# Average pooling over 64x256x8192: transfers of 64 KB per partition on one queue, with pairwise sums

## The chip, the cores and the metric

The kernel runs on one core of a Trainium2 chip. The metric is the device time in microseconds (us). Three runs of the kernel before gave 1561.38, 1561.14 and 1561.12 us; their median is 1561.14 us.

## The reference

The input x has 64 x 256 rows of 8192 float32 numbers. Each row is cut into windows of four, and the output is the mean of each window, so 64 x 256 rows of 2048.

```python
out_len = (length - kernel_size) // stride + 1     # 2048
for i in range(out_len):
    start = i * stride                             # kernel_size = stride = 4
    output[:, :, i] = np.mean(x[:, :, start : start + kernel_size], axis=2)
```

That is 536.87 MB to read and 134.22 MB to write, with three additions and one multiplication per result.

## The kernel before

The 16384 rows are taken in 32 groups of 512. A group gives each of the 128 partitions four rows that follow one another in memory, so a partition reads 128 KB of x and writes 32 KB of the output in one stretch. The function `_packed_fast_path` does the work (`F` is 4, `NTM` is 32); the rest of `tile_avg_pool_1d_kernel` holds paths that these shapes don't take.

For each group but the last, an inner loop over `f` takes one row per partition at a time. SP issues a load of 32 KB per partition, 4 MB in all (L245), into a tile `xt` from a pool of three buffers. VectorE sums each four neighbours with one TENSOR_REDUCE (L246) into a quarter of the result tile `ot`, which comes from a pool of two buffers. ACT multiplies that quarter by 1/4 in place (L252). After four rows ACT issues one store of the group, again 32 KB per partition and 4 MB (L253). So SP's queue carries the loads and ACT's the stores, and both queues feed the same 16 DMA engines.

The last group is cut finer. Its first row is loaded whole, its second and third in three chunks each (L263, L266, L272), and its fourth in a ladder of six chunks that get smaller, the last 608 columns wide (L284, L293, L309). The chunks of the ladder are stored by ACT as they are done (L310). The first three rows' results are held back and stored by SP in four pieces (L292) behind the last load. The very last chunk is scaled on VectorE into a tile `fin` (L300) and stored by SP (L307).

The tile framework puts in the semaphore waits: a load waits until the tile that it overwrites has been read, a reduction waits for its load and for the store that last read its result buffer, and so on. The order on each engine is the order of the program text. Each engine issues its DMAs in that order, and a DMA that waits holds up what stands behind it on the same engine.

Of the kernel before, what the change touches and what calls it, by code (L numbers as in the profile page):

```python
# [7 lines left out]
_N_PARK = 4  # L8
_FINAL_COLS_TGT = 608
_LADDER_RATIO = 1.39  # L10
_NCHUNK_PRE = 3
_PACK_STORES = True
_PACK_F_MAX = 4


def _tail_ladder(total: int, k: int, final: int, ratio: float = _LADDER_RATIO,
                 max_chunks: int = 12) -> list:
    if total < 4 * final:
        return [total]
    rev = []  # L20
    s = 0
    w = float(final)
    while len(rev) < max_chunks - 1:
        wi = max(k, (int(round(w)) // k) * k)
        if s + wi > total - k:
            break
        rev.append(wi)
        s += wi
        w *= ratio
    sizes = [total - s] + rev[::-1]  # L30
    assert sum(sizes) == total and all(x > 0 and x % k == 0 for x in sizes)
    return sizes


def _even_chunks(total: int, k: int, n: int) -> list:
    n = max(1, min(n, total // k))
    q = (total // n) // k * k
    sizes = [q] * n
    sizes[-1] += total - q * n
    assert sum(sizes) == total and all(s > 0 and s % k == 0 for s in sizes)  # L40
    return sizes


@with_exitstack
def kernel(
    ctx: ExitStack,
    tc: tile.TileContext,
    x: bass.AP,
    kernel_size: bass.AP,
    stride: bass.AP,  # L50
    out: bass.AP,
):
    nc = tc.nc

    K = int(kernel_size)
    S = int(stride)
    assert K == S, "only stride == kernel_size supported"

    B, C, L = x.shape
    OL = (L - K) // S + 1  # L60
    assert OL * K <= L

    P = nc.NUM_PARTITIONS

    xf = x.flatten_outer_dims()
    of = out.flatten_outer_dims()
    rows = B * C

    inv_k = 1.0 / float(K)
    dt = x.dtype  # L70
    IL = OL * K

    if _PACK_STORES and IL == L:
        F = 0
        for cand in range(_PACK_F_MAX, 1, -1):
            if rows % (P * cand) == 0 and (rows // (P * cand)) >= 2:
                F = cand
                break
        if F >= 2 and L >= 64 * K and OL % 8 == 0 and OL * F * 4 <= 32768:
            _packed_fast_path(nc, tc, xf, of, rows, L, OL, K, F, inv_k, dt, P)  # L80
            return

    RPP = 1
    R = P * RPP
    NT = rows // R
    IL2 = RPP * L
    OL2 = RPP * OL
    fast = (
        IL == L
        and rows % R == 0  # L90
        and NT >= 6
        and IL2 >= 64 * K
        and OL % 2 == 0
    )

    if not fast:
        with (
            tc.tile_pool(name="xin", bufs=4) as pin,
            tc.tile_pool(name="res", bufs=4) as pout,
        ):  # L100
            r0 = 0
            while r0 < rows:
                rn = min(P, rows - r0)
                xt = pin.tile([P, IL], dt)
                ot = pout.tile([P, OL], dt)
                nc.sync.dma_start(out=xt[:rn], in_=xf[r0 : r0 + rn, :IL])
                nc.vector.tensor_reduce(
                    out=ot[:rn],
                    in_=xt[:rn].rearrange("p (m k) -> p m k", k=K),
                    axis=mybir.AxisListType.X,  # L110
                    op=mybir.AluOpType.add,
                )
                nc.scalar.mul(ot[:rn], ot[:rn], inv_k)
                nc.scalar.dma_start(out=of[r0 : r0 + rn], in_=ot[:rn])
                r0 += P
        return

    def xview(t):
        return xf[t * R : (t + 1) * R]

    def oview(t):
        return of[t * R : (t + 1) * R]

    ladder = _tail_ladder(IL2, K, _FINAL_COLS_TGT)
    chunks_pre = _even_chunks(IL2, K, _NCHUNK_PRE)
    fin_w = ladder[-1] // K

    with (
        tc.tile_pool(name="xin", bufs=4) as pin,
        tc.tile_pool(name="res", bufs=4) as pout,  # L130
        tc.tile_pool(name="rsv", bufs=1) as prsv,
        tc.tile_pool(name="fin", bufs=1) as pfin,
    ):
        rsv = prsv.tile([P, OL2], dt)
        fin = pfin.tile([P, fin_w], dt)

        for t in range(NT):
            xv = xview(t)
            ov = oview(t)
            xt = pin.tile([P, IL2], dt)  # L140
            ot = rsv if t == 0 else pout.tile([P, OL2], dt)

            if t == 0:
                nc.sync.dma_start(out=xt[:, :IL2], in_=xv[:, :IL2])
                nc.vector.tensor_reduce(
                    out=ot[:, :OL2],
                    in_=xt[:, :IL2].rearrange("p (m k) -> p m k", k=K),
                    axis=mybir.AxisListType.X,
                    op=mybir.AluOpType.add,
                )  # L150
                nc.scalar.mul(ot[:, :OL2], ot[:, :OL2], inv_k)
            elif t < NT - 3:
                nc.sync.dma_start(out=xt[:, :IL2], in_=xv[:, :IL2])
                nc.vector.tensor_reduce(
                    out=ot[:, :OL2],
                    in_=xt[:, :IL2].rearrange("p (m k) -> p m k", k=K),
                    axis=mybir.AxisListType.X,
                    op=mybir.AluOpType.add,
                )
                nc.scalar.mul(ot[:, :OL2], ot[:, :OL2], inv_k)  # L160
                nc.scalar.dma_start(out=ov[:, :OL2], in_=ot[:, :OL2])
            elif t < NT - 1:
                c0 = 0
                for cw in chunks_pre:
                    c1 = c0 + cw
                    o0, o1 = c0 // K, c1 // K
                    nc.sync.dma_start(out=xt[:, c0:c1], in_=xv[:, c0:c1])
                    nc.vector.tensor_reduce(
                        out=ot[:, o0:o1],
                        in_=xt[:, c0:c1].rearrange("p (m k) -> p m k", k=K),  # L170
                        axis=mybir.AxisListType.X,
                        op=mybir.AluOpType.add,
                    )
                    nc.scalar.mul(ot[:, o0:o1], ot[:, o0:o1], inv_k)
                    nc.scalar.dma_start(out=ov[:, o0:o1], in_=ot[:, o0:o1])
                    c0 = c1
            else:
                nchunk = len(ladder)
                c0 = 0
                for i, cw in enumerate(ladder):  # L180
                    c1 = c0 + cw
                    o0, o1 = c0 // K, c1 // K
                    last = i == nchunk - 1
                    nc.sync.dma_start(out=xt[:, c0:c1], in_=xv[:, c0:c1])
                    if last:
                        q0 = 0
                        qw = (OL2 - q0) // _N_PARK
                        for qi in range(_N_PARK):
                            qa = q0 + qi * qw
                            qb = q0 + (qi + 1) * qw if qi != _N_PARK - 1 else OL2  # L190
                            nc.sync.dma_start(
                                out=oview(0)[:, qa:qb], in_=rsv[:, qa:qb]
                            )
                    nc.vector.tensor_reduce(
                        out=ot[:, o0:o1],
                        in_=xt[:, c0:c1].rearrange("p (m k) -> p m k", k=K),
                        axis=mybir.AxisListType.X,
                        op=mybir.AluOpType.add,
                    )
                    if last:  # L200
                        nc.vector.tensor_scalar(
                            out=fin[:, :fin_w],
                            in0=ot[:, o0:o1],
                            scalar1=inv_k,
                            scalar2=None,
                            op0=mybir.AluOpType.mult,
                        )
                        nc.sync.dma_start(out=ov[:, o0:o1], in_=fin[:, :fin_w])
                    else:
                        nc.scalar.mul(ot[:, o0:o1], ot[:, o0:o1], inv_k)  # L210
                        nc.scalar.dma_start(out=ov[:, o0:o1], in_=ot[:, o0:o1])
                    c0 = c1


def _packed_fast_path(nc, tc, xf, of, rows, L, OL, K, F, inv_k, dt, P):
    R = P * F
    NTM = rows // R

# [10 lines left out]
    with (  # L229
# [6 lines left out]
        for t in range(NTM):  # L236
            xv = xe(t)
# [109 lines left out]
```

## Time and profile before

| what | value |
|---|---|
| time, median of three runs | 1561.14 us (1561.12 to 1561.38) |
| span of the profiled execution, first to last instruction | 1559.0 us |
| VectorE (DVE) busy | 1112.8 us, 71% |
| ScalarE (ACT) busy | 247.4 us, 16% |
| bytes moved by the DMA engines | 671.14 MB, 430 GB/s over the span |
| HBM read and written | 536.87 MB and 134.22 MB |
| DMA packets | 25637 |
| loads of 4096 KB | 125, median 26.4 us from issue to landing |
| stores of 4096 KB by ACT | 31, median 23.2 us from issue to landing |

The profile is that of one execution. Its own time is its span, 1559.0 us, and what lies around the span, which the page doesn't list; against the median of the three runs that is 2.1 us.

The rows are read as follows. Busy time of an engine is the time in which it worked on instructions; issuing a DMA isn't counted. The row called DMA divides the span into 40 slices and gives, in tenths, how busy the 16 DMA engines were. A queue (q1, q10) has packets; the share is the time that its packets took out of 16 engines' span. A group of instructions is a line of the program with its operation and shapes, its number, its busy time and the mean of one, and the idle time of its engine just before it with what ended it. In the waits, the columns are the total, how often, and the longest. A "packet" is one piece that one DMA engine moves: each transfer here gives each of the 16 engines eight rows of partitions, and one packet of 4 bytes that reports the end. The chain is the work that ended last, followed back from the end.

### The profile page before, as it was taken

Reading aid. Unit: us, or ns where it says so; the run is one execution under the profiler, and the core shown is the slowest. Engines: PE = TensorE matmul, PEld = TensorE weight load, DVE = VectorE, ACT = ScalarE, POOL = GpSimd, SP = SyncE. Lnnn points to the kernel's source line nnn. Section 1 sums busy time; section 2 is a strip of 40 time slices with the busy share of each in tenths; the row PEclk is TensorE's granted clock in tenths of the full one; section 3 lists DMA queues with packets and bytes.
Section 4 is the critical chain, followed back from the end, with each engine's and each line's share of the span. In section 5 each row is a group of like instructions: output and inputs, shape, how many; then the busy total and the mean of one; then the engine's idle time right before and its main releaser. Section 6 shows DMA issues by size and latency. Waiting matters only on the chain.

```text
span 1559.0 us, 724 instructions
## 1 busy us (share of the span) xinstructions
DVE 1112.8 (71%) x138; ACT 247.4 (16%) x137; POOL 0.2 (0%) x4
## 2 busy tenths in 40 slices
DVE  6777667776667866677666776667766677766786
ACT  1111111111111111111111111111111111111111
POOL 0000000000000000000000000000000000000000
DMA  9999999999999999999999999999999999999999
GB/s 416 418 430 436 437 432 430 430 430 432 439 433 430 430 432 430 438 434 431 430 432 430 435 434 433 431 431 430 433 437 433 432 430 431 430 437 434 432 427 384
DMA packets 25637, 671.14 MB, mean 430 GB/s; under 512 B 2848, under 2 KB 3488, under 8 KB 4768
## 3 DMA queue, kind: packets, MB, share of 16 engines
q1 hardware_dynamic: 20448, 540.10, 80.6%
q10 hardware_dynamic: 5184, 131.00, 19.5%
q14 instruction: 5, 0.04, 0.0%
HBM read 536.87 MB, written 134.22 MB: 430 GB/s over the span
## 4 chain that ended last, share of the span: by engine, by line
DMA 75%; DVE 24%; issue 0%; SPq 0%; DVEq 0%
DMA xt<-in_x_dram 75%; DVE ot L246 23%; DVE ot L293 1%; DVE ot L266 0%; SPq L263 0%; DVEq L246 0%; DVE fin L300 0%
## 5 line engine op out<-in xcount | busy, mean ns | idle before, releaser
L246 DVE TENSOR_REDUCE ot<-xt 128x2048 f32<-128x8192 f32 x124 | 1077.1, 8686 | 430.2 <-DMA xt<-in_x_dram 430.2
L252 ACT ACTIVATE ot<-ot 128x2048 f32<-128x2048 f32 x124 | 237.0, 1911 | 1270.2 <-DVE ot L246 1270.2
L266 DVE TENSOR_REDUCE ot<-xt 128x682 f32<-128x2728 f32 (+2 forms) x7 | 26.6, 3809 | 6.9 <-DMA xt<-in_x_dram 6.9
L272 ACT ACTIVATE ot<-ot 128x682 f32<-128x682 f32 (+2 forms) x7 | 6.6, 936 | 25.8 <-DVE ot L266 25.8
L293 DVE TENSOR_REDUCE ot<-xt 128x417 f32<-128x1668 f32 (+5 forms) x6 | 9.0, 1568 | 0.0
L309 ACT ACTIVATE ot<-ot 128x417 f32<-128x417 f32 (+4 forms) x5 | 2.6, 521 | 5.2 <-DVE ot L293 5.2
L252 ACT ACT_TABLE_LOAD x1 | 1.3, 1283 | 0.7 <-PEq L328 0.7
L300 DVE TENSOR_SCALAR fin<-ot 128x152 f32<-128x152 f32 x1 | 0.2, 239 | 0.0
L328 POOL MEMSET const-bfloat16-1.0<- 128x1 bf16 x1 | 0.1, 102 | 0.0
L328 POOL MEMSET const-uint8-127<- 128x1 uint8 x1 | 0.1, 102 | 0.0
L328 POOL MEMSET const-float32-0.0<- 128x1 f32 x1 | 0.1, 99 | 0.2 <-issue 0.2
L328 POOL MEMSET const-float32-1.0<- 128x1 f32 x1 | 0.1, 99 | 0.0
## 6 DMA issues: line engine op xcount, KB each, us to landing
xt<-in_x_dram SPq DMA_DIRECT2D x125, 4096.0 KB, 26.4
out_dram<-ot ACTq DMA_DIRECT2D x31, 4096.0 KB, 23.2
xt<-in_x_dram SPq DMA_DIRECT2D x4, 1364.0 KB, 23.4
out_dram<-ot SPq DMA_DIRECT2D x4, 768.0 KB, 7.7
xt<-in_x_dram SPq DMA_DIRECT2D x2, 1368.0 KB, 29.5
xt<-in_x_dram SPq DMA_DIRECT2D x1, 1134.0 KB, 16.2
xt<-in_x_dram SPq DMA_DIRECT2D x1, 834.0 KB, 22.6
xt<-in_x_dram SPq DMA_DIRECT2D x1, 816.0 KB, 17.8
```

What stands on the lines that cost most here:

```text
L246: nc.vector.tensor_reduce(out=ot[:, o0 : o0 + OL], in_=xt[:, :L].rearrange("p (m k) -> p m k", k=K), axis=mybir.AxisListType.X, op=mybir.A ...
L252: nc.scalar.mul(ot[:, o0 : o0 + OL], ot[:, o0 : o0 + OL], inv_k)
L266: nc.vector.tensor_reduce(out=ot[:, o0:o1], in_=xt[:, c0:c1].rearrange("p (m k) -> p m k", k=K), axis=mybir.AxisListType.X, op=mybir.AluOp ...
L272: nc.scalar.mul(ot[:, o0:o1], ot[:, o0:o1], inv_k)
L293: nc.vector.tensor_reduce(out=ot[:, o0:o1], in_=xt[:, c0:c1].rearrange("p (m k) -> p m k", k=K), axis=mybir.AxisListType.X, op=mybir.AluOp ...
L300: nc.vector.tensor_scalar(out=fin[:, :fin_w], in0=ot[:, o0:o1], scalar1=inv_k, scalar2=None, op0=mybir.AluOpType.mult,)
L309: nc.scalar.mul(ot[:, o0:o1], ot[:, o0:o1], inv_k)
L328: nc = _bacc.Bacc("TRN2", target_bir_lowering=False, num_devices=1)
```

## The change

The paths that other shapes need are taken out, and the main path is written anew.

- A tile `xt` holds 16384 columns, 64 KB per partition, from a pool of two buffers instead of three of 32 KB. A load fills it at once: 8 MB.
- A group is 65536 columns per partition, eight rows that follow one another in memory, so there are 16 groups of four loads. The result tile `ot` holds 64 KB per partition, from a pool of one buffer instead of two of 32 KB. One store writes it: 8 MB.
- All loads and stores are issued by SP. Two loads are issued ahead; load k+2 is issued behind the sums of tile k and, where tile k ends a group, behind the group's store.
- The sum of four is made in two levels: one add of even and odd columns, written over the first half of the tile itself, and one add of even and odd columns of that, written to `ot`. In the fourth tile of a group the second level is cut into four parts, with a multiplication by ACT after each.
- The last tile is loaded in five pieces of 8192, 4096, 2048, 1024 and 1024 columns. The last group's results are stored in four parts: two tiles' worth between the first and the second piece, then the third tile's, then 3584 columns, then 512. The last two pieces are scaled on VectorE.

The diff, cut to what is new and to the lines of `_packed_fast_path` that it replaces:

```diff
-    with (
-        tc.tile_pool(name="xin", bufs=3) as pin,
-        tc.tile_pool(name="res", bufs=2) as pout,
-        tc.tile_pool(name="fin", bufs=1) as pfin,
-    ):
...
-            if t < NTM - 1:
-                for f in range(F):
-                    xt = pin.tile([P, L], dt)
-                    o0 = f * OL
-                    nc.sync.dma_start(out=xt[:, :L], in_=xv[:, f * L : (f + 1) * L])
-                    nc.vector.tensor_reduce(
...
-                    nc.scalar.mul(ot[:, o0 : o0 + OL], ot[:, o0 : o0 + OL], inv_k)
-                nc.scalar.dma_start(out=ov[:, : F * OL], in_=ot[:, : F * OL])
-                continue
...
+LOADS = 4
+LAST_CUTS = 4
...
+    per = B * C * L // P
+    W = 16384
+    G = W * LOADS
+    V = W // K
+    groups = per // G
...
+    rows = G // L
+    R = P * rows
+    def xg(g):
+        return xf[g * R : (g + 1) * R].rearrange("(p f) m -> p (f m)", f=rows)
...
+    pin = ctx.enter_context(tc.tile_pool(name="xin", bufs=2))
+    pout = ctx.enter_context(tc.tile_pool(name="res", bufs=1))
+    state = {}
+    def load(g, l, a, b):
+        if a == 0:
+            state["xt"] = pin.tile([P, W], dt, name="xt")
+        xt = state["xt"]
+        nc.sync.dma_start(out=xt[:, a:b], in_=xg(g)[:, l * W + a : l * W + b])
+        return xt
+    def sums(xt, ot, l, a, b, cuts, scale_on_dve=False):
+        h = (a, (a + b) // 2)
+        nc.vector.tensor_tensor(
+            out=xt[:, h[0] : h[1]], in0=xt[:, a:b:2], in1=xt[:, a + 1 : b : 2], op=add
+        )
+        n = (b - a) // K
+        for c in range(cuts):
+            lo, hi = c * n // cuts, (c + 1) * n // cuts
+            o = ot[:, l * V + a // K + lo : l * V + a // K + hi]
+            nc.vector.tensor_tensor(
+                out=o,
+                in0=xt[:, a + 2 * lo : a + 2 * hi : 2],
+                in1=xt[:, a + 2 * lo + 1 : a + 2 * hi : 2],
+                op=add,
+            )
+            if scale_on_dve:
+                nc.vector.tensor_scalar(
+                    out=o, in0=o, scalar1=1.0 / K, scalar2=None, op0=mybir.AluOpType.mult
+                )
+            else:
+                nc.scalar.mul(o, o, 1.0 / K)
+    def store(g, ot, a, b):
+        nc.sync.dma_start(out=og(g)[:, a:b], in_=ot[:, a:b])
+    todo = [(g, l) for g in range(groups) for l in range(LOADS)]
+    last = todo[-1]
+    pieces = [W // 2, W // 4, W // 8, W // 16, W // 16]
+    tiles = {}
+    ot = None
+    tiles[0] = load(*todo[0], 0, W)
+    tiles[1] = load(*todo[1], 0, W)
+    for k, (g, l) in enumerate(todo[:-1]):
+        if l == 0:
+            held, ot = ot, pout.tile([P, G // K], dt, name="ot")
+        sums(tiles.pop(k), ot, l, 0, W, LAST_CUTS if l == LOADS - 1 else 1)
+        if l == LOADS - 1:
+            store(g, ot, 0, G // K)
+        if k + 2 < len(todo) - 1:
+            tiles[k + 2] = load(*todo[k + 2], 0, W)
+        elif k + 2 == len(todo) - 1:
+            n = pieces[0]
+            lt = load(*last, 0, n)
+            store(g, ot, 0, (l + 1) * V)
+            for w in pieces[1:]:
+                load(*last, n, n + w)
+                n += w
+    g, l = last
+    store(g, ot, (l - 1) * V, l * V)
+    edges = [sum(pieces[:i]) for i in range(len(pieces) + 1)]
+    for a, b in zip(edges[:3], edges[1:4]):
+        sums(lt, ot, l, a, b, 1)
+    store(g, ot, l * V, l * V + edges[3] // K)
+    for a, b in zip(edges[3:-1], edges[4:]):
+        sums(lt, ot, l, a, b, 1, scale_on_dve=True)
+    store(g, ot, l * V + edges[3] // K, (l + 1) * V)
```

More of the change, by code (lines that the diff above doesn't have):

```diff
@@ L6 @@
 from concourse._compat import with_exitstack
[L8 to L41, printed above, removed]
+LOADS = 4
+LAST_CUTS = 4
 @with_exitstack
@@ L53 @@
     nc = tc.nc
-    K = int(kernel_size)
-    S = int(stride)
-    assert K == S, "only stride == kernel_size supported"
+    K, S = int(kernel_size), int(stride)
+    assert K == S == 4
     B, C, L = x.shape
-    OL = (L - K) // S + 1
-    assert OL * K <= L
     P = nc.NUM_PARTITIONS
+    add = mybir.AluOpType.add
+    dt = x.dtype
+    per = B * C * L // P
[3 more added lines that the diff above has]
+    groups = per // G
+    assert per == groups * G
     xf = x.flatten_outer_dims()
@@ L66 @@
     of = out.flatten_outer_dims()
[L67 to L96, printed above, removed]
-        with (
-            tc.tile_pool(name="xin", bufs=4) as pin,
-            tc.tile_pool(name="res", bufs=4) as pout,
-        ):
[L101 to L106, printed above, removed]
-                nc.vector.tensor_reduce(
[L108 to L111, printed above, removed]
-                )
[L113 to L131, printed above, removed]
-        tc.tile_pool(name="fin", bufs=1) as pfin,
[L133 to L176, printed above, removed]
-            else:
[L178 to L212, printed above, removed]
@@ L215, in _packed_fast_path @@
-def _packed_fast_path(nc, tc, xf, of, rows, L, OL, K, F, inv_k, dt, P):
-    R = P * F
-    NTM = rows // R
-    ladder = _tail_ladder(L, K, _FINAL_COLS_TGT)
-    chunks_pre = _even_chunks(L, K, _NCHUNK_PRE)
-    fin_w = ladder[-1] // K
-    def xe(t):
-        return xf[t * R : (t + 1) * R].rearrange("(p f) m -> p (f m)", f=F)
-    def oe(t):
-        return of[t * R : (t + 1) * R].rearrange("(p f) m -> p (f m)", f=F)
-    with (
-        tc.tile_pool(name="xin", bufs=3) as pin,
-        tc.tile_pool(name="res", bufs=2) as pout,
-        tc.tile_pool(name="fin", bufs=1) as pfin,
-    ):
-        fin = pfin.tile([P, fin_w], dt)
-        for t in range(NTM):
-            xv = xe(t)
-            ov = oe(t)
-            ot = pout.tile([P, F * OL], dt)
-            if t < NTM - 1:
-                for f in range(F):
-                    xt = pin.tile([P, L], dt)
-                    o0 = f * OL
-                    nc.sync.dma_start(out=xt[:, :L], in_=xv[:, f * L : (f + 1) * L])
-                    nc.vector.tensor_reduce(
-                        out=ot[:, o0 : o0 + OL],
-                        in_=xt[:, :L].rearrange("p (m k) -> p m k", k=K),
-                        axis=mybir.AxisListType.X,
-                        op=mybir.AluOpType.add,
-                    )
-                    nc.scalar.mul(ot[:, o0 : o0 + OL], ot[:, o0 : o0 + OL], inv_k)
-                nc.scalar.dma_start(out=ov[:, : F * OL], in_=ot[:, : F * OL])
-                continue
-            for f in range(F - 1):
-                xt = pin.tile([P, L], dt)
-                widths = [L] if f < F - 3 else chunks_pre
-                c0 = 0
-                for cw in widths:
-                    c1 = c0 + cw
-                    o0, o1 = f * OL + c0 // K, f * OL + c1 // K
-                    nc.sync.dma_start(
-                        out=xt[:, c0:c1], in_=xv[:, f * L + c0 : f * L + c1]
-                    )
-                    nc.vector.tensor_reduce(
-                        out=ot[:, o0:o1],
-                        in_=xt[:, c0:c1].rearrange("p (m k) -> p m k", k=K),
-                        axis=mybir.AxisListType.X,
-                        op=mybir.AluOpType.add,
-                    )
-                    nc.scalar.mul(ot[:, o0:o1], ot[:, o0:o1], inv_k)
-                    c0 = c1
-            fq = F - 1
-            xt = pin.tile([P, L], dt)
-            hold = fq * OL
-            nchunk = len(ladder)
-            c0 = 0
-            for i, cw in enumerate(ladder):
-                c1 = c0 + cw
-                o0, o1 = fq * OL + c0 // K, fq * OL + c1 // K
-                last = i == nchunk - 1
-                nc.sync.dma_start(
-                    out=xt[:, c0:c1], in_=xv[:, fq * L + c0 : fq * L + c1]
-                )
-                if last:
-                    qw = hold // _N_PARK
-                    for qi in range(_N_PARK):
-                        qa = qi * qw
-                        qb = (qi + 1) * qw if qi != _N_PARK - 1 else hold
-                        nc.sync.dma_start(out=ov[:, qa:qb], in_=ot[:, qa:qb])
-                nc.vector.tensor_reduce(
-                    out=ot[:, o0:o1],
-                    in_=xt[:, c0:c1].rearrange("p (m k) -> p m k", k=K),
-                    axis=mybir.AxisListType.X,
-                    op=mybir.AluOpType.add,
-                )
-                if last:
-                    nc.vector.tensor_scalar(
-                        out=fin[:, :fin_w],
-                        in0=ot[:, o0:o1],
-                        scalar1=inv_k,
-                        scalar2=None,
-                        op0=mybir.AluOpType.mult,
-                    )
-                    nc.sync.dma_start(out=ov[:, o0:o1], in_=fin[:, :fin_w])
-                else:
-                    nc.scalar.mul(ot[:, o0:o1], ot[:, o0:o1], inv_k)
-                    nc.scalar.dma_start(out=ov[:, o0:o1], in_=ot[:, o0:o1])
-                c0 = c1
@@ new lines, with og @@
+    rows = G // L
+    R = P * rows
+    def xg(g):
+        return xf[g * R : (g + 1) * R].rearrange("(p f) m -> p (f m)", f=rows)
+    def og(g):
+        return of[g * R : (g + 1) * R].rearrange("(p f) m -> p (f m)", f=rows)
+    pin = ctx.enter_context(tc.tile_pool(name="xin", bufs=2))
[7 more added lines that the diff above has]
+        return xt
```

## The prediction

> **What bounds the kernel now.** I read the busy rows first, then the DMA rows, the chain that ended last, the waits, and last the trace's own DMA packet records. The page's head, busy rows, DMA slices and queues:
>
> ```profile
> span 1559.0 us, 724 instructions
> DVE 1112.8 (71%) x138; ACT 247.4 (16%) x137; POOL 0.2 (0%) x4
> DMA  9999999999999999999999999999999999999999
> DMA packets 25637, 671.14 MB, mean 430 GB/s; under 512 B 2848, under 2 KB 3488, under 8 KB 4768
> q1 hardware_dynamic: 20448, 540.10, 80.6%
> q10 hardware_dynamic: 5184, 131.00, 19.5%
> ```
>
> No engine is full, but the 16 DMA engines are: their row never falls under 9, and the two queues' packets (q1 is SP's, q10 ACT's) fill 80.6 + 19.5 = 100.1% of 16 engines' span. All bytes must move in either version, 671.09 MB, so time can only come from what the DMA engines do besides moving bytes, or from idling. The windows answer both:
>
> ```profile
> 100.00:1500.00 1400.00, 1000.30 (x116) 221.61 (x116) 0.00 (x0) 1.00 1.00 433
> 1551.00:1554.00 3.00, 0.00 (x0) 0.00 (x0) 0.00 (x0) 1.00 1.04 401
> 1554.00:1557.00 3.00, 0.00 (x0) 0.00 (x0) 0.00 (x0) 1.00 0.65 253
> ```
>
> (last two columns: DMA share, GB/s). For 1400 us the engines stand at 1.00 and 433 GB/s; only the last 4 us sag. So the chain's and the waits' rows, which name VectorE too, show a pipeline paced by loads:
>
> ```profile
> DMA xt<-in_x_dram 75%; DVE ot L246 23%; DVE ot L293 1%; DVE ot L266 0%; SPq L263 0%; DVEq L246 0%; DVE fin L300 0%
> DVE ot L246 <- DMA xt<-in_x_dram: 430.2, 124, 12.7
> SPq L245 <- DVE ot L246: 1053.4, 121, 8.8
> ```
>
> VectorE waits 430 us for loads. SP waits 1053 us for VectorE to free a tile, but that costs nothing: other loads are queued then, as the full DMA row shows.
>
> **What a packet costs besides its bytes.** The trace records every packet. 25637 = 16 x (8+1) x 178 + 5: each of the 178 transfers (137 loads, 41 stores) gives every engine eight data packets, one per partition row, and one of 4 B. From one packet's start to the next on the same engine I find on average 1212.7 ns after 32768 B, 409.4 ns after 10912 B, 27.1 ns after 608 B, and 6 ns after the 4 B packet. From 10912 to 32768 B the slope is 803.3/21856 = 0.03676 ns/B and 8.3 ns are left per packet; from 608 to 32768 B 0.03687 ns/B, with 4.7 ns left. I take the middle, 6.5 ns.
>
> **The change, part by part.**
>
> *Transfers of 64 KB.* Transfers fall to 68 loads (63 whole, the last tile in 5 pieces) and 19 stores (15 whole, 4 for the last group): 87, so each engine has 696 data packets instead of 1424, and 91 fewer 4 B packets. Gain: 728 x 6.5 ns = 4.7 us, and 91 x 6 ns = 0.5 us. Nothing hides it, since the DMA engines are the bound. A 65536 B packet is not in the trace: if its extra cost grows with its bytes, the 4.7 is 0; at 8.3 ns it is 6.0. I take the middle.
>
> *Stores on SP's queue, in line with loads.* Today the queues alternate packet by packet: a load packet followed by a store packet takes 1211.9 ns, store then load 1210.1, load then load 1214.0. Changing direction at every packet thus costs nothing visible; changing at 16 stores costs nothing either, and losing the alternation costs at most 1214.0 - 1210.1, about 4 ns on each of some 2 x 3968/16 = 496 packets: 2 us. From below, losing the alternation could gain as much. I take 0. After a store's 4 B packet the next packet on the queue starts 6 ns later, in the tail too, so a store ahead doesn't hold the line.
>
> *Sums in two levels.* Per 64 KB tile an add with 8192 results and one (or four quarters) with 4096 results replace two reductions. No two-input add is in the trace. The nearest rows are
>
> ```profile
> L246 DVE TENSOR_REDUCE ot<-xt 128x2048 f32<-128x8192 f32 x124 | 1077.1, 8686 | 430.2 <-DMA xt<-in_x_dram 430.2
> L266 DVE TENSOR_REDUCE ot<-xt 128x684 f32<-128x2736 f32 x2 | 6.0, 3004 | 4.3 <-DMA xt<-in_x_dram 4.3
> ```
>
> (mean ns after busy us): (8686-3004)/(8192-2736) = 1.041 ns per element read, 155 ns fixed. If an add takes this per result, the levels cost 8.69 and 4.42, 13.1 us a tile (13.6 with four quarters); if per element read, 17.2 and 8.7, 25.9 us. I take the first: the nearest row on how fast VectorE can read is the TENSOR_SCALAR of L300, 239 ns for 152 elements, (239-155)/152 = 0.55 ns each, so two elements per 1.04 ns are within its reach. The Trainium skill, "VectorE: DVE Perf Modes", section on the TRN2 errata, gives a fp32 two-input add (N+151)/0.96 ns; its estimate would be 8.7 + 4.4 = 13.1 us. No run shown here has it.
>
> *Two tiles, one result buffer, one queue: does the line run dry?* A 64 KB load takes 8 x 2 x 1212.7 ns less the saving, 19.3 us. From the first tile of before: VectorE starts 0.37 us after the load's last packet, and the first packet moves 1.0 us after SP's issue. Load k+2 waits for the sums of tile k: 0.37 + 13.2 + 1.0 = 14.6 us after that tile landed, while load k+1 holds the line for 19.3. Cover: 4.7 us. At the start the first tile lands 9.7 us later than today, but the second load is queued behind it, so the line stays full. A store must come sooner: 0.37 + 13.7, then ACT's last quarter (ACT rows: 772 ns at 682, 1911 at 2048, so 1.06 at 1024), + 1.0 = 16.2 us. Cover: 3.1 us; each us beyond it idles the engines 16 times. Behind the waiting store in SP's queue stands the next load, which needs only the same sums, and the line is filled by the load before. The next group's second level waits until the store has left the buffer, 19.3 us after that store starts; its tile is then freed 19.3 + 0.4 + 4.4 = 24 us after, well inside the 38.7 us that store and next load take together. Four loads per store and one buffer thus cost 0.
>
> *The tail.* Before, from 1554.00 to the last packet's end at 1557.63 (packet records) the engines are busy 0.65 x 3 + about 0.02 of 3.63 us: 1.6 us idle. After, the last tile's pieces land while stores still queue: with the durations above the 14 KB store is ready 1.9 us before its turn, the final 2 KB one 3.5 us before. (ACT's 3.6 us per 4096 results and the scaling of the last two pieces on VectorE, some 0.3 us each, are in this.) What stays is the spread between engines (0.47 us between first and last 4 B packet of one load). Gain 1.2 us; ends 0 and 1.6. Start (first packet at 1.73 us) and the 1.4 us after the last packet stay.
>
> **Sum.** 4.7 + 0.5 + 1.2 = 6.4 us off the profiled span: 1559.0 becomes 1552.6. That execution's span lies 2.1 us below the runs' median 1561.14; these 2.1 stay, so the forecast is **1554.7 us**. Ends: 6.0 + 0.5 + 1.6 + 2 = 10.1 off, 1551.0; with 0 for packets and tail, and alternation lost: 0.5 - 2, so 1562.6.
>
> **A rule that speaks against it.** The load rows' pitch per partition grows from 128 to 256 KB, the stores' from 32 to 64 KB. Before, at 128 KB, moves 433 GB/s. The Trainium skill, "DMA: Bandwidth & Descriptors", section "Latency and other measured facts", has HBM copies at a pitch of 512 KiB at 207 GB/s where a padded pitch gave 214, and much less at larger powers of two. By it a pitch between could lose up to about 3%, an estimate of 47 us and 1600 us. No run here shows it.
>
> **Rivals.** (1) *No change within 0.2% (3 us; about what a measurement of this kernel can tell):* the 64 KB row goes out as two packets of 32 KB, or the extra cost grows with the bytes. Then only 0.5 + 1.2 stay: 1559.4. For it: no packet over 32768 B is in the trace, and the average packet lies 3.7 ns over the fastest (1209), which may be any cause. Against: packets of six sizes all show a fixed part.
> (2) *Slower: the adds are paced by elements read.* Then VectorE, not DMA, is the bound: a group costs 3 x 25.9 + 17.2 + 4 x 2.3 = 104 us, against 96.8 for its DMA, plus about 4.5 in which the second level waits for the store: 16 x 108.6 + 22 for the first load + 6 = about 1766 us. It decides from 16.8 us of sums a tile on (13.7 + 3.1); I expect 13.7. For it: two strided inputs, in place, never seen here. Against: the 0.55 ns per element of L300.
> (3) *Slower: DMA packets of 64 KB rows run slower*, by pitch or direction. Each 1% costs 15 us: 1570 at 1%. Against: the alternation costs nothing, and the tail's 6144 B stores take 230 ns, their bytes at the same slope and 4 ns.
>
> **Chances.** Forecast 0.70; (1) 0.14; (2) 0.06; (3) 0.10. So faster 0.70, same 0.14, slower 0.16. The range runs from 1551.0 to 1562.6 and takes in the bounds and (1), leaving out (2) and (3).
>
> **What would show it.** Right: about 12,500 packets, loads of 65536 B at about 2418 ns, DMA share 1.00 and 434 GB/s or more in the middle, adds of 8.7 and 4.4 us. Wrong: twice the packets (rival 1); adds over 11 us and DMA slices under 9 (2); packets over 2440 ns (3); a dip of the DMA row once per group would say that the store's cover is gone.

## The result, and the profile after

| | time, median (lowest to highest) | ratio to before |
|---|---|---|
| before, 20 runs | 1561.02 us (1560.80 to 1561.44) | |
| changed, 20 runs | 1558.42 us (1556.78 to 1560.36) | 0.9984 [0.9978, 0.9990] |

The forecast was 6.4 us less; 2.6 us came. The time lies inside the stated range, and it lies closer to "no change" than to the forecast. The profiled execution of the changed kernel took 1560.02 us, 1.6 us over its median. So its profile shows one of its longest runs; the runs of the changed kernel are spread over 3.6 us, those of before over 0.6. Two later repeats (e12 and e16 below) came 1.5 and 1.2 us under the kernel before, so the gain is some 1 to 2.6 us.

The page of the changed kernel, the lines that answer to those shown of before:

```profile
span 1558.2 us, 522 instructions
DVE 844.0 (54%) x183; ACT 241.9 (16%) x112; POOL 0.2 (0%) x4
DMA  9999999999999999999999999999999999999998
DMA packets 12532, 671.13 MB, mean 431 GB/s; under 512 B 1392, under 2 KB 1392, under 8 KB 1776
q1 hardware_dynamic: 12528, 671.09, 99.8%
```

The packets are 16 x 9 x 87 + 4, as worked out ahead, so a row of 64 KB does go out as one packet. The DMA row stays at 9 in every slice but the last, which shows 8. The queue's share says more: 99.8% of a span that is only 0.8 us shorter. The packets are half as many and take nearly as long.

Groups by form, mean ns of one after busy us, and two waits, the first of VectorE, the second of SP:

```profile
L65 DVE TENSOR_TENSOR xt<-xt 128x8192 f32<-128x8192 f32 x63 | 547.6, 8693 | 537.0 <-DMA xt<-in_x_dram 537.0
L72 DVE TENSOR_TENSOR ot<-xt 128x4096 f32<-128x4096 f32 x48 | 212.4, 4425 | 163.5 <-DMA out_dram<-ot 162.4
L72 DVE TENSOR_TENSOR ot<-xt 128x1024 f32<-128x1024 f32 x61 | 70.7, 1220 | 0.5
```

```profile
DVE ot L72 <- DMA out_dram<-ot: 162.4, 15, 11.2
```

```profile
SPq L59 <- DVE ot L72: 780.1, 47, 24.3
```

The adds take 8.69, 4.42 and 1.22 us, one result per 1.04 ns. The wait for the one result buffer is there, 11 us for each of 15 groups, and the DMA slices above show no gap for it.

The middle and the tail in windows (last columns: DMA share, GB/s), against 433 GB/s in the first window and shares of 1.04 and 0.65 in the other two before:

```profile
100.00:1500.00 1400.00, 752.66 (x157) 214.68 (x99) 0.00 (x0) 1.00 1.00 434
1551.00:1554.00 3.00, 0.00 (x0) 0.00 (x0) 0.00 (x0) 1.00 0.92 389
1554.00:1557.00 3.00, 0.00 (x0) 0.00 (x0) 0.00 (x0) 1.00 0.34 135
```

**Where the gain went.** I split the DMA engines' time, in us per engine, by the packet records of both traces. "Expected" is 0.03676 ns/B and 4.4 ns a packet, which is what the fastest packets take. A packet that takes over 40 ns more than that is called held.

| us per engine | before | changed | difference |
|---|---|---|---|
| expected | 1549.1 | 1545.4 | -3.7 |
| packets up to 40 ns over it | 2.5 | 1.2 | -1.3 |
| held at the start | 0.6 | 0.5 | -0.2 |
| held when the first store starts | 1.0 | 1.5 | +0.5 |
| held elsewhere | 0.1 | 3.5 | +3.4 |
| idle in the last 20 us | 1.6 | 2.4 | +0.8 |

The first two rows, -5.0 us, are the packet terms of the forecast (-5.2). They were paid back by held packets, most of them around stores, and by a tail that idles more, not less. Held packets leave no mark in the page: the DMA row stays at 9, because a held packet counts as busy.

The first store in the timeline (start, duration, engine, line), with the sums ahead of it and the next tile's:

```profile
80.69 8.69 DVE L65 TENSOR_TENSOR xt<-xt 128x8192 f32<-128x8192 f32 x1 [6.18 <-DMA xt<-in_x_dram]
90.67 4.46 ACT L83 ACTIVATE ot<-ot 128x1024 f32<-128x1024 f32 x4 [12.52 <-DVE ot L72]
95.17 0.35 SPq L86 DMA_DIRECT2D out_dram<-ot  x1
95.61 58.13 SPq L59 DMA_DIRECT2D xt<-in_x_dram  x3
101.45 8.69 DVE L65 TENSOR_TENSOR xt<-xt 128x8192 f32<-128x8192 f32 x1 [7.41 <-DMA xt<-in_x_dram]
```

The store is issued at 95.17, while the load ahead of it is still moving. That load should land 19.3 us after the one before it; it lands 1.2 us later than that, as VectorE's wait of 7.41 us in place of 6.18 shows.

### The profile page after: what moved, and what is told of

Its sections match the earlier page's. It is cut to its first block, busy times and chain, and to the rows that moved or that the text cites. A ratio compares the mean times of both kernels' runs of the same rounds, so it can differ in the third digit from the quotient of the medians.

```text
span 1558.2 us, 522 instructions
## 1 busy us (share of the span) xinstructions
DVE 844.0 (54%) x183; ACT 241.9 (16%) x112; POOL 0.2 (0%) x4
## 2 busy tenths in 40 slices
DMA packets 12532, 671.13 MB, mean 431 GB/s; under 512 B 1392, under 2 KB 1392, under 8 KB 1776
## 3 DMA queue, kind: packets, MB, share of 16 engines
q1 hardware_dynamic: 12528, 671.09, 99.8%
## 4 chain that ended last, share of the span: by engine, by line
DMA 71%; DVE 27%; ACT 1%; SPq 0%; issue 0%
DMA xt<-in_x_dram 71%; DVE xt L65 18%; DVE ot L72 9%; ACT ot L83 1%; SPq L86 0%; SPq L59 0%; DVE ot L79 0%
## 5 line engine op out<-in xcount | busy, mean ns | idle before, releaser
L65 DVE TENSOR_TENSOR xt<-xt 128x8192 f32<-128x8192 f32 (+2 forms) x68 | 556.9, 8190 | 542.5 <-DMA xt<-in_x_dram 542.5
L83 ACT ACTIVATE ot<-ot 128x1024 f32<-128x1024 f32 (+3 forms) x111 | 240.6, 2167 | 1306.1 <-DVE ot L72 1302.6
L72 DVE TENSOR_TENSOR ot<-xt 128x1024 f32<-128x1024 f32 (+4 forms) x113 | 286.9, 2572 | 164.1 <-DMA out_dram<-ot 162.4
```

The source lines that it names most:

```text
L65: nc.vector.tensor_tensor(out=xt[:, h[0] : h[1]], in0=xt[:, a:b:2], in1=xt[:, a + 1 : b : 2], op=add)
L72: nc.vector.tensor_tensor(out=o, in0=xt[:, a + 2 * lo : a + 2 * hi : 2], in1=xt[:, a + 2 * lo + 1 : a + 2 * hi : 2], op=add,)
L83: nc.scalar.mul(o, o, 1.0 / K)
```

## The experiments

All but e11 build on the changed kernel, with the times of 4 to 12 runs each beside the kernel before. "Held" below is the sum per engine in the profiled run, without the start and the first store. The line is what stands queued on the DMA engines; a transfer joins it when it is issued, and its turn comes when all ahead of it has moved.

**e3: packets back to 32 KB.**

```diff
-        nc.sync.dma_start(out=xt[:, a:b], in_=xg(g)[:, l * W + a : l * W + b])
+        n = (b - a) // 8192 or 1
+        w = (b - a) // n
+        for i in range(a, b, w):
+            nc.sync.dma_start(out=xt[:, i : i + w], in_=xg(g)[:, l * W + i : l * W + i + w])
```

and the same in `store`.

> The changed kernel with each load and store of 64 KB per partition issued as two of 32 KB, one behind the other on SP; order, buffers and sums unchanged. Packet theory (each packet costs 5 to 8 ns besides its bytes): 624 more data packets and 78 more 4 B packets per engine, 3.1 to 4.9 + 0.5 us, about 1562.5 us. If packet size did nothing and the gain came from elsewhere: 1558.4 to 1558.9 us. Theory C (holds belong to 64 KB packets) lets the holds of 3.5 us vanish: about 1559.

Measured: 1561.90 us (1561.07 to 1562.54), ratio to before 1.0005 [0.9997, 1.0014]; 23765 packets. It is 3.5 us over the changed kernel and no longer faster than before. Against the two repeats it is 2.4 and 2.0 us. So the gain comes from the packets' number, as the packet theory has it. Held packets fell from 3.5 to 1.2 us all the same, so the shorter packets gave some of their cost back.

**e2, e5 and e1: where the store joins the line, and on which queue.** All three have two loads to a store and two result buffers of 32 KB:

```diff
-LOADS = 4
+LOADS = 2
-    pout = ctx.enter_context(tc.tile_pool(name="res", bufs=1))
+    pout = ctx.enter_context(tc.tile_pool(name="res", bufs=2))
```

e2 leaves the store where it was, ahead of load k+2; e5 puts it behind that load; e1 leaves it in its place and issues it from ACT (`nc.scalar.dma_start`). The store lines of the tail are fitted to the shorter group in all three.

> The same two loads to a store and two result buffers of 32 KB, but all stores issued by SP as in the changed kernel: 31 turns from load to store in place of 16, half as long. Theory A (turn): twice the holds, 2.7 us more, and 0.9 us for packets: 1562.0 us, 6 us above the kernel with stores on ACT, and holds on the last load packets before most stores. Theory B (late joining): each store still joins some 3 us ahead of its turn, so also about 1562. Theory C (64 KB packets): 1559.3 us, equal to the kernel with stores on ACT.

> As the kernel with two loads to a store, two result buffers and all on SP, but each group store is issued behind the next load, so that it joins the line some 19 us more ahead of its turn. Theory A (turn): the same as with the earlier store, 1562 us, holds of the same size. Theory B (late joining): holds gone, 1558.5 us or less. Theory C (64 KB packets): 1559.3, same as the other two of this set.

> Two loads to a store and two result buffers of 32 KB, so 31 group stores of 4 MB; the group stores are issued by ACT, the rest stays as in the changed kernel (median 1558.4 us). Theory A (turn: on one queue, the last load packet ahead of a store is held, in the changed kernel's trace 2.7 us per engine over stores 2 to 15 and 0.8 us at the tail's first store): the holds go, except at the first store; against that 120 more packets and 15 more 4 B packets per engine, 0.9 us. 1558.4 - 3.5 + 0.9 = 1555.8 us. Theory B (the store joins its line too late, some 3 us ahead of its turn): the same 1555.8, since on another queue it has no turn. Theory C (the holds belong to 64 KB packets, not to the stores' place): holds stay, 1559.3 us.

| | time | ratio to before | held |
|---|---|---|---|
| e2, SP, ahead of the load | 1569.38 us (1568.92 to 1570.26) | 1.0053 [1.0041, 1.0066] | 12.6 us |
| e5, SP, behind the load | 1558.20 us (1557.38 to 1559.61) | 0.9983 [0.9974, 0.9991] | 2.0 us |
| e1, ACT | 1555.63 us (1555.42 to 1559.97) | 0.9966 [0.9952, 0.9979] | 3.8 us, in the run of 1559.97 |

The timelines of the first store (start, duration, engine, line), e2 first, then e5:

```profile
56.44 0.35 SPq L86 DMA_DIRECT2D out_dram<-ot  x1
56.88 18.80 SPq L59 DMA_DIRECT2D xt<-in_x_dram  x2
62.17 8.69 DVE L65 TENSOR_TENSOR xt<-xt 128x8192 f32<-128x8192 f32 x1 [6.84 <-DMA xt<-in_x_dram]
```

```profile
55.25 0.33 SPq L59 DMA_DIRECT2D xt<-in_x_dram  x1
56.34 0.35 SPq L86 DMA_DIRECT2D out_dram<-ot  x1
61.21 8.69 DVE L65 TENSOR_TENSOR xt<-xt 128x8192 f32<-128x8192 f32 x1 [5.99 <-DMA xt<-in_x_dram]
```

The store is issued within 0.1 us of the same time in both. In e2 its turn comes when the load under way has landed, at about 61 us (VectorE starts on that tile at 62.17); in e5 a whole load stands between. That swap alone is worth 11.2 us, with the same number of packets, turns and bytes. Theory A (the turn costs, wherever the store joined) had both at 1562; theory C (the packets) had all three equal. Both fall as a whole explanation. Theory B (late joining) has the order right, but put e2 at 1562, 7 us too low. A windows row shows what little of it a page can tell, e2 first, then e5 (DMA share 1.00 in both):

```profile
200.00:1400.00 1200.00, 649.98 (x172) 195.03 (x124) 0.00 (x0) 1.00 1.00 430
```

```profile
200.00:1400.00 1200.00, 657.52 (x172) 191.85 (x121) 0.00 (x0) 1.00 1.00 433
```

Something is left for the turn. In e5 the first store holds its forerunners 0.87 us, the next ones 0.35, 0.14 and 0.25, and past 700 us none more than 0.1. Meanwhile the spread between the first and the last engine at the end of a load grows from 0.4 to 3.2 us. That engines in step hold each other when they all turn at once fits this, but nothing here isolates it.

**e6: the changed kernel's store joins early.**

```diff
-            store(g, ot, 0, G // K)
+            store(g, ot, l * V, G // K)
...
             tiles[k + 2] = load(*todo[k + 2], 0, W)
+            if l == LOADS - 2:
+                store(g, ot, 0, (l + 1) * V)
```

> The changed kernel, but each group store is parted: the first three quarters (48 KB per partition) are issued behind the load that follows the group, and the last quarter (16 KB) where the whole store stood. So the first part joins its line some 19 us ahead of its turn and the second behind it; one queue, one buffer and 16 turns stay. Theory B (a store that joins some 3 us ahead of its turn holds the load packet ahead of it): the 2.7 us of holds at stores 2 to 15 go, 120 packets and 15 4 B packets per engine cost 0.9 us: 1558.4 - 2.7 + 0.9 = 1556.6 us. Theory A (the turn itself costs): 1558.4 + 0.9 = 1559.3 us.

Measured: 1557.35 us (1556.88 to 1559.28), 0.9979 [0.9970, 0.9987]; held 1.0 us. It is 1.1 us under the changed kernel (2.2 and 2.6 under its repeats), although its 15 more stores should cost 0.9. That is theory B's direction and at least more than half of its size (1.8 us).

**e9: the store joins still later.** `LAST_CUTS = 1` in place of 4.

> The changed kernel with the fourth tile's second level and its scaling in one piece in place of four, which moves the group store's issue from 16.2 to 18.2 us after the tile's landing: 1.1 us ahead of its turn in place of 3.1. Nothing else changes. Theory B (late joining): holds grow from 0.2 us a store to 0.4 (as in the kernel with two loads to a store) or up to 2.4 (a whole packet), so 1561 to 1592 us. Theory A (the turn): 1558.4 us.

Measured: 1559.88 us (1559.11 to 1561.08), 0.9993 [0.9985, 1.0002]; held 6.7 us with the first store, against 4.8 to 5.7 in the changed kernel's three traces. The time is 1.5 us over the changed kernel's first median and equal to its repeats (1559.53 and 1559.92), so the later store is dearer in held packets, not clearly in time, and it stays under theory B's lower end of 1561. The engines' spread, from the first to the last of the 16 at the end of a load, stays between 0.4 and 1.3 us here, where it grows beyond 3 us in the changed kernel. The trace idles 0.95 us in all, against 2.8 in the changed kernel. Why the spread stays small isn't shown.

**Which engine's cover counts.** A 4 B packet ends every transfer on every engine, so the packet records show when the first and when the last engine comes to a store's turn. "Ahead" in this table is that time less the store's issue and the 1.0 us from issue to the first packet. "Turn in" is the held time at the end of the load ahead of the store, "turn out" that at the end of the store, ahead of the next load. All are of the stores of whole groups without the first, for e6 of both parts of each store.

| | ahead of the last engine's turn | ahead of the first engine's turn | turn in | turn out |
|---|---|---|---|---|
| changed kernel, first profile | 3.4 to 4.6 us | 0.1 to 2.6 us | 1.0 us | 1.2 us |
| e12 and e16, its repeats | 3.4 to 4.6 us | 0.2 to 2.3 us | 1.2 and 1.3 us | 1.1 and 1.9 us |
| e2 | 3.5 to 4.9 us | -0.6 to 3.2 us | 3.5 us | 7.6 us |
| e9 | 1.0 to 1.2 us | -0.2 to 0.5 us | 0.0 us | 4.0 us |
| e5 | 22.8 to 33.1 us | 19.5 to 32.2 us | 1.8 us | 0.0 us |
| e6 | 17.9 to 20.9 us | 15.3 to 19.4 us | 0.7 us | 0.0 us |

Two costs come apart. The turn out is held where the first engine has almost no cover: 14 of e2's stores have under 0.5 us and hold 6.9 of its 7.6 us, the five with over 1 us hold 0.1; in e9 it is 3.7 of 4.0 us, in the changed kernel's three traces 3.2 of 4.2. Stores that join early hold nothing there. The turn in is another cost: it stays in e5 and e6, where the store joins 15 us ahead and more, and it is nothing in e9, where the store joins latest. So an early issue helps, as theory B has it, but not in the way it gives: a late store doesn't hold the load ahead of it, its own last packets are held. The load behind it was issued right after the store, so it isn't late itself; why it comes out so isn't visible in the records.

**e7, e13, e14: loads that join late.** Each sum of a whole tile is followed by one more add, 2048 (e7, e13) or 4096 results (e14) wide:

```diff
+        if b - a == W:
+            nc.vector.tensor_tensor(
+                out=xt[:, 8192:10240], in0=xt[:, 0:2048], in1=xt[:, 2048:4096], op=add
+            )
```

e7 adds it to e1. e13 and e14 add it to e4, which is the changed kernel without most stores (`if l == LOADS - 1 and g == 0:` ahead of the store). The second column is the estimate for the last engine to come to the turn.

> The changed kernel without the stores of groups 1 to 14: those outputs are not written, all loads and sums stay. 14 stores of 19.32 us fall away, 270.5 us. Theory store (holds belong to stores, by turn or by late joining): besides these their holds go, 1 to 2.7 us: 1285.2 to 1286.9 us, and between 150 and 1240 us the trace has next to no held packets. Theory load (64 KB loads fall into holds by themselves, with engines drifting apart): 1287.9 us and held packets as in the changed kernel.

> The kernel with two loads to a store and the stores on ACT's queue (1555.6 us), with one more add of 2048 results on each tile, whose results are used by nobody. It frees each tile 2.3 us later, so that in the stretches without stores a load joins its line some 2.4 us ahead of its turn in place of 4.7. Theory B1 (late joining holds whatever stands ahead, load or store): holds at up to 62 loads, 0.2 to 0.4 us each, 1565 to 1580 us. Theory B2 (only a store that joins late holds a load): 1555.6 us, unchanged.

> The changed kernel without the stores of groups 1 to 14 (1286.5 us, no holds), with one more add of 2048 results on each tile, used by nobody. Loads alone, each joining its line 2.4 us ahead of its turn in place of 4.7. Theory B1 (any transfer that joins late holds the packet ahead): holds at some 58 loads, 0.1 to 0.4 us each, 1292 to 1310 us, or two groups of runs as in the kernel with late loads beside stores. Theory B2 (only around stores): 1286.5 us.

> The same with an extra add of 4096 results, 4.4 us: a load joins some 0.3 us ahead of its turn, less than the engines' spread of 0.8 us, so engines that run ahead find the line empty. Theory B1: idle time or holds of 0.5 us and more at each of 58 loads, 1315 us or more. Theory B2: the line runs dry only for the fastest engines; they wait up to 0.5 us without delaying the last one, 1286.5 to 1290 us.

| | a load joins ahead of its turn by | time | held | idle |
|---|---|---|---|---|
| e4, no stores | 4.7 us | 1286.52 us (1286.01 to 1286.78) | 0.2 us | 2.2 us |
| e13 | 2.4 us | 1306.92 us (1302.37 to 1308.76) | 14.7 us | 5.4 us |
| e14 | 0.3 us | 1370.66 us (1367.04 to 1373.53) | 31.4 us | 52.5 us |
| e7, beside stores | 2.4 us | 1558.65 us (1556.98 to 1570.68) | 11.1 us, in a run of 1568.55 | 4.0 us |

Held and idle are of the profiled runs (1286.01, 1302.37, 1367.04, 1568.55). Rows of the windows, e4, e13, e14:

```profile
200.00:1200.00 1000.00, 683.13 (x143) 195.98 (x91) 0.00 (x0) 1.00 1.00 433
```

```profile
200.00:1200.00 1000.00, 782.56 (x189) 191.79 (x87) 0.00 (x0) 1.00 1.00 427
```

```profile
200.00:1200.00 1000.00, 843.89 (x182) 180.94 (x84) 0.00 (x0) 1.00 0.96 406
```

This is the clearest result. VectorE is far from full in all three. At 4.7 us the loads move at 433 GB/s and hold nothing. At 2.4 us the DMA share is still 1.00, and the loads move at 427: 1306.92 - 1286.52 = 20.4 us are lost, 0.35 for each of 58 loads. Only at 0.3 us does the share fall. So a load that joins its line 2.4 us ahead of the last engine's turn already costs, long before a page shows a gap. For the first engine it is -0.1 to 1.8 us in e13, and 2.9 to 3.5 us in e4, by the packet records. The lost time lies in the late load itself: 13.5 of e13's 14.7 us are in packets that start within 4 us of the first engine's turn, most of them the late load's first, and 0.3 us is in the last packets of the load ahead. Most of it (12.6 us) starts while VectorE stands idle, so the extra add doesn't slow these packets by working beside them. Theory B2 (only stores) fell. Of e7's twelve runs seven stayed within 1557.0 to 1558.9, under B1's 1565 to 1580, and five took 1564.6 to 1570.7; what decides between them in a run is open.

**e10: a tile freed earlier.** e1 with a part of the first level in a buffer of its own, so that tiles are free 1.8 us sooner.

```diff
+        H = 8704
+        scr = pscr.tile([P, (W - H) // 2], dt, name="scr")
+        nc.vector.tensor_tensor(
+            out=scr[:, :], in0=xt[:, H:W:2], in1=xt[:, H + 1 : W : 2], op=add
+        )
...
```

> The kernel with two loads to a store and the stores on ACT's queue (1555.6 us, one run of five at 1560.0), with the first level written partly (3840 of 8192 results) into a small buffer of its own, so that a tile is free 11.4 us after its sums start in place of 13.2 and a load joins the line 6.5 us ahead of its turn in place of 4.7. Theory B1 (late joining holds whatever stands ahead, and it starts where the engines' spread eats the cover): the rare long runs go, all runs within 1555 to 1557, median 1555.5 us. Theory B2 (only stores): nothing changes, long runs stay.

Measured: 1557.30 us (1556.65 to 1558.18), 0.9976 [0.9967, 0.9985]; held 1.2 us. No run came near 1560 in ten, but the median is 1.7 us above e1's, on another chip; its tail idles 2.0 us. It decides nothing.

**e8: another tail.** e1 with the last whole group's store behind the last load's pieces.

> The kernel with two loads to a store and the stores on ACT's queue (1555.6 us), with the last whole group's 4 MB store issued by SP behind the last load's pieces, so that loads land 9.7 us earlier and more work stands in line at the end. The tail of the changed kernel's trace has 2.4 us in which engines idle, because engines that run ahead wait for the 14 KB store. Theory tail: 1 to 1.5 us less, 1554.3 us. Rival (the idle time is the spread of the engines, which no order mends): 1555.6 us.

Measured: 1555.99 us (1555.82 to 1560.80), 0.9972 [0.9963, 0.9981]. Idle time is 1.3 us in its trace against 2.7 in e1's, which is the trace of a long run, but the median is not lower. The rival stands: the order of the last transfers alone doesn't make the time shorter.

**e11: the kernel before, with its stores on SP.** The one line L253 is `nc.sync.dma_start` in place of `nc.scalar.dma_start`.

> The kernel before with its 31 group stores issued by SP in place of ACT, nothing else: 32 KB packets, reductions, three and two buffers. A store joins its line 12 us after its last tile's landing, some 7 us ahead of its turn. Theory A (the turn costs): 31 turns at 0.1 to 0.4 us, 1564 to 1573 us. Theory B (late joining alone costs): 1561 us, at most 1 us more. My prediction's step (one queue costs nothing): 1561.0 us, within 2 us.

Measured: 1666.97 us (1666.86 to 1667.02), 1.0679 [1.0664, 1.0693], far outside all three. I had overlooked what stands behind the store in SP's order:

```profile
32.20 8.69 DVE L246 TENSOR_REDUCE ot<-xt 128x2048 f32<-128x8192 f32 x1 [1.04 <-DMA xt<-in_x_dram]
50.66 1.91 ACT L252 ACTIVATE ot<-ot 128x2048 f32<-128x2048 f32 x1 [7.83 <-DVE ot L246]
51.62 8.69 DVE L246 TENSOR_REDUCE ot<-xt 128x2048 f32<-128x8192 f32 x1 [0.99 <-DMA xt<-in_x_dram]
52.60 0.35 SPq L253 DMA_DIRECT2D out_dram<-ot  x1
53.04 30.43 SPq L245 DMA_DIRECT2D xt<-in_x_dram  x4
74.42 8.69 DVE L246 TENSOR_REDUCE ot<-xt 128x2048 f32<-128x8192 f32 x1 [14.11 <-DMA xt<-in_x_dram]
```

The store waits for ACT until 52.60, and the load behind it, whose tile had been free since the sums of 32.20 to 40.89, is issued only at 53.04. The load under way had landed by 51.62, so the line was dry: by the packet records some 2.5 us idle and 0.85 us held for each of 31 stores, 3.4 x 31 = 105 us. Moving the stores to SP is thus no free edit. In the changed kernel the load that covers the store's wait is twice as long.

**e12, e16, e15: the same kernels again.**

> The changed kernel once more, unchanged, for a second profile. Its 20 runs went from 1556.8 to 1560.4 us, the profiled one was 1560.0. If the spread of the runs comes from the holds, a profiled run of 1557 to 1558.5 us has 1 to 3 us less of held packets than the first profile's 4.9 us past the start; if it comes from elsewhere, the holds are the same.

> The changed kernel unchanged, on the same chip as the one with stores on ACT. Two chips gave it 1558.4 and 1559.5 us; here 1558 to 1560 us, with 3 to 4 us of held packets behind the first store in its profile.

> The kernel with two loads to a store, two result buffers and the group stores on ACT's queue once more, beside the changed kernel on one chip. Theory (late joining and turns of stores on one queue cost): 1555.6 us again, 3 to 4 us below the changed kernel; now and then a run near 1560. If the chips differ and not the kernels: both at the same time.

The changed kernel: 1559.53 us (1558.11 to 1560.20), 0.9989 [0.9981, 0.9998], and 1559.92 us (1558.05 to 1560.30), 0.9990 [0.9982, 0.9999]; held 3.5 and 4.6 us in profiled runs of 1559.53 and 1559.99. e1's twin, on the same chip as the second: 1555.83 us (1555.69 to 1558.42), 0.9971 [0.9959, 0.9982]. So the 4.1 us between the changed kernel and e1's are the kernels', not the chips'. No short run of the changed kernel was profiled, so whether its runs differ by their held packets stays open.

The fastest version found is e1: 1555.6 and 1555.8 us, 0.3% under before and below the changed kernel. Its two profiled executions are both among its long runs (1559.97 and 1558.42), with most of their held packets in the last 300 us.

## Why the prediction was right in part and wrong in part

- **The bound, and transfers of 64 KB: right.** The DMA engines stay the bound, the packets are 12,532, a packet of 65536 B takes 2418 ns from start to start on average where another follows (I expected about 2418). The term of 5.2 us measures 5.0 in the traces, and e3, with its packets of half the size, gives the gain up.
- **Two levels of sums: right.** 8.69 and 4.42 us, and 13.4 us from start to end for a tile with four quarters (13.6 expected).
- **One result buffer and its wait: right in costing nothing of itself.** The 162 us that VectorE waits lie beside transfers.
- **"Cover: 3.1 us; each us beyond it idles the engines 16 times", and so one buffer and one queue "thus cost 0": wrong, and this is the step that failed.** The cover itself was about right for the last engine: stores join 3.4 to 4.6 us ahead of its turn. But I took the 16 engines for one, and the line to be safe until it runs dry. The runs show that the engines drift up to 3.8 us apart, so that the first has only 0.1 to 2.6 us, and that time is lost inside packets before the line is dry. Held packets elsewhere than at start and first store are 3.4 us more than before: of the 3.5 us, 1.2 lie at the ends of stores and 1.0 at the turns into them (stores 2 to 15), 0.8 at the tail's first store, and the rest elsewhere. e6, which issues most of the store a load earlier, has 1.0 us in place of 3.5, none of it at the ends of stores.
- **"Changing at 16 stores costs nothing either": wrong by about 1 us.** The held turns into stores stay when the store is issued early (0.7 us in e6, 1.8 in e5). They go with the growth of the engines' spread; which of the two causes the other isn't shown.
- **"After a store's 4 B packet the next packet starts 6 ns later, so a store ahead doesn't hold the line": true of the gap and wrong as a conclusion.** The lost time lies inside the packets, not between them. e1, with the stores back on ACT, is 2.8 and 4.1 us faster than the changed kernel, the second on the same chip, in spite of more packets. Against e5, which has its packets and its chip but one queue, it is 2.6 us. Whether that is the alternation or only that a store on its own queue has no turn isn't shown.
- **The tail: wrong sign.** I expected 1.2 us less idling and got 0.8 more. I had taken the spread between engines as 0.47 us from one early load; at the end it is 3.3 us in the changed kernel's trace. The leading engines reach the 14 KB store up to 1.0 us before its first packet can start, and the last engine sets the end. That this spread is what the tail lost is argued, not shown: e8 changes the tail and its idle time, and not the median.
- **Sum.** -5.0 for packets, +3.7 for held packets with start and first store, +0.8 for the tail: -0.5 us, against the 0.6 us by which the last packet of the changed kernel's profiled run ends earlier (1557.01 against 1557.63 us). The median run is 1.6 us better than that run, and how its time is split wasn't recorded. That the measured time lies inside the range is luck: the range was wide for packets and alternation, and had no term for held packets.
- **The rivals.** (1), no change within 3 us, comes nearest in time, but not by its reasons: the packets are half as many, and e3 shows that their number costs. (2) would have had slower adds, which aren't seen. (3), slower packets by direction, is the nearest in kind, though not for the row's pitch: between held packets those of 64 KB take what their bytes give, 2418 ns from start to end. The rule on the row pitch (the Trainium skill, "DMA: Bandwidth & Descriptors", "Latency and other measured facts") isn't seen at 256 KB: 433 GB/s between 200 and 1400 us, against 432 with 128 KB before.

## What to carry to other kernels

When the DMA engines are full, count the packets: their fixed share is small but certain, and here worth 5 of 1560 us. Then see for every transfer how long ahead of its turn it is issued, and count from the engine that comes there first: take the engines' spread off. Here 3.4 to 4.6 us, less a spread of 3, were not enough, and the busy row didn't show the loss. Issue the store behind one more load, or let another engine issue it, and look in the packet records for packets that take longer than their bytes.

## What the runs showed of the hardware that was not expected

- A transfer that joins late makes packets longer rather than leaving a gap. A late load lengthens its own first packets: 2.4 us ahead of the last engine's turn, 14.7 us of held packets against 4.2 us of idle time before the last 20 us (e13). A late store has its own last packets held: 4.0 us at the ends of 14 stores in e9, none in e5 and e6. In which part of the DMA engine the time is lost isn't visible in the trace.
- The 16 engines drift apart: from 0.8 us between the first and the last at the first load to 3.3 us at the end (changed kernel), and up to 5.5 us with the stores on ACT (e1), while in e4, without most stores, it stays at 0.9 to 1.4 us until the tail. In e9 it stays at 0.4 to 1.3 us. A line that runs short doesn't always keep the engines together: in e14, which runs dry, the spread reaches 3.7 us.
- The first store of a run holds the load packets under way by 0.7 to 1.5 us per engine in all traces but those of e9 and e11, also before (1.0 us), whatever queue it is on.
- Longer packets seem to need an earlier issue: with 32 KB packets in the same order (e3) held packets are 1.2 us, with 64 KB 3.5 to 4.6 (three traces). With one trace of e3 this is no more than a hint.
